# A mixing layer computed with seven block products per output pair instead of eight, its weight parts prepared one stage earlier

## The chip, the cores and the metric

The kernel runs on one core of one Trainium2 chip. The core has TensorE (PE: matrix products into PSUM), VectorE (DVE), ScalarE (ACT), GpSimd (POOL) and SyncE (SP, which here only issues DMAs). The metric is the device time of one execution in microseconds. The kernel before takes 1331.76 us, the median of three runs (1331.52 to 1332.87).

## The reference

One decoder layer over 1024 tokens of width 1024, in float32:

```python
xn = rmsnorm(x, norm_mix_w)
proj = xn @ w_in                       # q, k, v of both attentions, two gates
y_da = diff_attention(...)             # (1024, 512)
y_sw = sliding_window_attention(...)   # (1024, 512)
merged = sigmoid(g_da) * (y_da @ w_br_da) + sigmoid(g_sw) * (y_sw @ w_br_sw)
x = x + merged @ w_mix_out             # the mixing layer: 1024 x 1024 x 1024
xn = rmsnorm(x, norm_ffn_w)
x = x + conv_ffn(xn, w_up, conv_w, conv_b, w_down)   # width 2816
return rmsnorm(x, norm_final_w)
```

The change touches the mixing layer, `merged @ w_mix_out`, the merge just before it and the first step of the up projection just after it.

## The kernel before, in words

Everything is kept transposed: a tile has 128 channels on the partitions and up to 1024 tokens along the free dimension, so the width of 1024 makes eight tiles. TensorE works on float32r operands. To keep float32 accuracy each factor is split into a high part (a cast on ACT, float32 to float32r) and a low part (a subtraction on DVE, value minus high part), and each product of two blocks costs three matmuls: high x high, high x low, low x high.

Large products are mostly computed with a seven-product scheme (Strassen-Winograd form): both factors are cut into 2 x 2 blocks, sums and differences of blocks are formed, seven block products are computed instead of eight, and the results are recombined. The input projection, the up projection (`hidden`) and the down projection (`down`) do this. In the down projection the sums of weight blocks are formed by DMA: a tile `S` is loaded on SP's queue, negated on ACT (L108) where needed, and further quarters are added to it by an accumulating DMA on POOL's queue (L91). The mixing layer before the change uses plain products.

**The merge** (`rest`, from L781). Eight input tiles `y` from the two attentions are split. Then, for each output tile m = 0..7 (loop at L802): the branch weights of tile m are taken from a queue of prepared weights (`next_w`, which keeps two sets: cast L156 on ACT, subtraction L158 on DVE); two gate tiles `gr` are loaded from DRAM (four buffers), multiplied by the norm factor on POOL (L808), put through the sigmoid on ACT (L815); TensorE computes both branches, 48 matmuls, into a two-bank tile `sc` and two one-bank tiles `g`; DVE multiplies them into the gates (L819, L824); POOL adds the two (L825; DVE for the last tile); ACT and DVE split the sum into `mh` and `ml` (L828, L829).

**The mixing layer** (`mix`, L842). For each of eight output tiles: the residual tile `x` is loaded, the split weights are taken from the queue, 48 matmuls go to `sc` (L177 to L179, `mm3`), DVE adds the residual (L867), the sum is stored for later use (`x2d`), ACT scales it by the next norm's weight (L870) and squares it (L879), POOL adds the squares up (L880). After every second tile, `operands` (L886) forms the block operands of the up projection from the pair of tiles k and k+4.

**The first step of the up projection** (`hidden`, L922). For j = 0 five of the seven products run over the first three k, then the last operands T4 and T2 are split, then the five products get their fourth k, with column sums of the squares behind them, and the remaining two products follow.

The order of the work on each engine is made by the framework's scheduler from the program order, priorities (`high_priority`) and the dependencies; each engine then runs its own list strictly in order, and so does each DMA queue. A tile pool with `bufs=n` lets n tiles of one tag live at the same time.

## Time and profile before

The profile is of one execution that took 1330.42 us, with a span of 1328.4 us from its first to its last instruction.

| | us | share of the span |
|---|---|---|
| one profiled execution | 1330.42 | |
| its span | 1328.4 | |
| TensorE busy | 1315.8 | 99% |
| VectorE busy | 1049.4 | 79% |
| ScalarE busy | 614.7 | 46% |
| GpSimd busy | 478.0 | 36% |
| the merge, 500 to 588 us: TensorE / VectorE / ScalarE / GpSimd busy | 88.0 / 47.2 / 33.4 / 57.2 | |
| the mixing layer, 588 to 675 us: the same | 87.0 / 52.1 / 34.0 / 24.3 | |

A row of the groups by line reads: line of the kernel, engine, operation, output <- inputs, shape, number of instructions | busy us in total, mean ns of one | idle us of the engine just before them, and what ended most of it. A row of the timeline reads: start in us, length in us, engine, line, operation, count, and in brackets the idle time before it and what ended it. A row of the chain reads: start, length, engine and line of the piece of work on the path that ended last. The rows of windows give for each stretch its length, then for PE, PEld, DVE, ACT and POOL the busy us with the number of instructions, then the granted clock, the mean busy share of the 16 DMA engines and GB/s. Matmuls are pipelined, so the length of one row is longer than the distance to the next.

### The profile page before, as it was taken

To read this page: it belongs to the slowest core of one execution; us is meant where nothing else is said; L and a number is where in the kernel's file an instruction comes from. 1 tells how busy PE (TensorE), PEld (TensorE's weight loads), DVE (VectorE), ACT (ScalarE), POOL (GpSimd) and SP (SyncE) were. 2 spreads that over 40 slices of the span, in tenths; PEclk is the share of its full clock that TensorE was granted. 3 is DMA by queue.
4 is the path that set the end of the run, shared out by engine and by line. 5 is a ranking of instruction groups with operands and counts; after the bars stand their busy time and mean duration, and the time that the engine had idled before them with its cause. 6 is when DMAs were issued, how large, how long until landed. Compare 5 with 4: busy or idle time off the path is not lost.

```text
span 1328.4 us, 17040 instructions
## 1 busy us (share of the span) xinstructions
PE 1315.8 (99%) x6264; PEld 1097.6 (83%) x6264; DVE 1049.4 (79%) x1431; ACT 614.7 (46%) x946; POOL 478.0 (36%) x364
## 2 busy tenths in 40 slices
PE   9999999999999999999999999999999999999997
PEld 7888888888888878888888888888888888888886
DVE  8846775289888976455669999999999997886654
ACT  9432232276667774333444443343434344345643
POOL 0446652001101015751435666665566631101111
PEclk9999999999999999999999999999999999999999
DMA  7334333966554236334422222122222228867532
GB/s 260 126 144 157 145 148 122 269 179 190 143 133 142 82 126 225 120 118 151 143 95 95 80 79 93 66 95 80 82 77 86 81 75 333 266 158 143 111 98 108
DMA packets 63234, 180.25 MB, mean 136 GB/s; under 512 B 6960, under 2 KB 16816, under 8 KB 63152
## 3 DMA queue, kind: packets, MB, share of 16 engines
q1 hardware_dynamic: 49120, 153.48, 35.1%
q0 software_dynamic: 2304, 8.39, 3.7%
q10 hardware_dynamic: 11728, 17.31, 3.6%
q8 instruction: 49, 0.80, 0.3%
q14 instruction: 33, 0.27, 0.1%
HBM read 130.39 MB, written 48.76 MB: 135 GB/s over the span
## 4 chain that ended last, share of the span: by engine, by line
PE 97%; ACT 1%; DVE 1%; DMA 0%; issue 0%; SPq 0%; POOLq 0%; POOL 0%; ACTq 0%
PE t L919 45%; PE y L1169 7%; PE d L1169 5%; PE g L177 4%; PE g L178 4%; PE g L179 4%; PE sc L177 3%; PE sc L179 3%; PE sc L178 3%; PE sc L651 3%; PE y L1120 2%; PE d L1120 2%; PE t L667 1%; PE t L770 1%; PE sc L739 1%; PE t L679 1%
## 5 line engine op out<-in xcount | busy, mean ns | idle before, releaser
L1063 POOL TENSOR_TENSOR us<-us,rstd 128x1024 f32<-128x1024 f32 x42 | 92.2, 2214 | 82.5 <-DVE us L484 47.6
L1072 ACT ACTIVATE c<-us,vecs 128x1024 f32<-128x1024 f32 x44 | 54.8, 1248 | 127.1 <-POOL us L1063 121.5
L137 DVE TENSOR_TENSOR sl<-sf,sh 128x1024 fp32r<-128x1024 f32 x62 | 89.3, 1441 | 12.8 <-ACT sh L135 12.8
L158 DVE TENSOR_TENSOR wl<-raw,wh 128x1024 fp32r<-128x1024 f32 (+1 forms) x49 | 68.0, 1389 | 35.5 <-ACT wh L156 25.9
L135 ACT CAST sh<-sf 128x1024 fp32r<-128x1024 f32 x62 | 64.6, 1044 | 62.1 <-PE t L919 44.0
L156 ACT CAST wh<-raw 128x1024 fp32r<-128x1024 f32 (+1 forms) x49 | 49.6, 1014 | 91.2 <-PE sc L178 33.4
L121 POOL TENSOR_TENSOR sf<-rv 128x512 f32<-128x512 f32 x30 | 50.4, 1679 | 99.5 <-DVE sl L137 59.0
L1169 PE MATMUL y<-h,wh 128*128 128x512 f32 (+1 forms) x288 | 80.8, 366 | 0.0
L1075 DVE SCALAR_TENSOR_TENSOR c<-us,vecs,c 128x1024 f32<-128x1024 f32 x44 | 78.5, 1817 | 0.0
L1074 DVE SCALAR_TENSOR_TENSOR c<-us,vecs,c 128x1024 f32<-128x1024 f32 x44 | 69.3, 1606 | 5.6 <-ACT c L1072 5.5
L123 POOL TENSOR_TENSOR sf<-raw,rv 128x512 f32<-128x512 f32 x30 | 56.7, 1890 | 46.6 <-DVE sl L137 46.6
L177 PE MATMUL g<-xh,wh 128*128 128x512 f32 x176 | 71.0, 404 | 1.5 <-ACT g L580 1.5
L178 PE MATMUL g<-xl,wh 128*128 128x512 f32 x176 | 70.3, 400 | 0.0
L179 PE MATMUL g<-xh,wl 128*128 128x512 f32 x176 | 70.2, 399 | 0.0
L1055 ACT ACTIVATE c<-c 128x1024 f32<-128x1024 f32 x22 | 23.4, 1063 | 83.4 <-DVE c L1075 83.4
L655 DVE CUSTOM_DVE_ANT_0 L<-sc,bias 128x128 f32<-128x128 f32 (+7 forms) x64 | 47.7, 752 | 17.0 <-PE sc L651 13.7
L634 POOL MEMSET aT<- 128x128 f32 x32 | 6.1, 204 | 151.8 <-PE t L680 98.0
L137 DVE TENSOR_TENSOR wl<-raw,wh 128x1024 fp32r<-128x1024 f32 (+1 forms) x32 | 59.7, 1864 | 0.1
L1169 PE MATMUL d<-h,wh 128*128 128x512 f32 x192 | 59.4, 390 | 0.0
L1169 PEld LDWEIGHTS y<-h,wh 128*128 128x128 f32 x288 | 52.1, 189 | 8.7
L122 POOL TENSOR_TENSOR sf<-sf,raw 128x512 f32<-128x512 f32 x31 | 58.2, 1878 | 2.2
L656 ACT ACTIVATE L<-L,sm 128x128 f32<-128x128 f32 (+7 forms) x64 | 49.6, 778 | 20.0 <-DVE sm L655 17.3
(411 smaller groups left out, 4255.4 us busy)
## 6 DMA issues: line engine op xcount, KB each, us to landing
u<-qd SPq DMA_DIRECT2D x72, 256.0 KB, 6.4
raw<-in_w_up SPq DMA_DIRECT2D x23, 512.0 KB, 3.5
raw<-in_w_in SPq DMA_DIRECT2D x22, 512.0 KB, 3.7
hd<-c SPq DMA_DIRECT2D x22, 512.0 KB, 2.6
rv<-in_w_up SPq DMA_DIRECT2D x21, 512.0 KB, 3.6
gr<-gd SPq DMA_DIRECT2D x16, 512.0 KB, 3.4
S<-in_w_down POOLq DMA_DIRECT2D x16, 512.0 KB, 6.7
qd<-us SPq DMA_DIRECT2D x15, 512.0 KB, 2.6
```

Of the source, the lines that this page charges most:

```text
L122: tt(sa[:, 1], sa[:, 0], g[:, 0], ALU.subtract)
L135: cast = nc.scalar.copy(hi, src)
L137: low = nc.vector.tensor_tensor(lo, src, hi.bitcast(F32), ALU.subtract)
L158: self.lo = (eng or nc.vector).tensor_tensor(wl, raw, wh.bitcast(F32), ALU.subtract)
L177: nc.tensor.matmul(ps, wh[:, kc + o, :], ah, start=first and n == 0, stop=False)
L178: nc.tensor.matmul(ps, wh[:, kc + o, :], al, start=False, stop=False)
L179: nc.tensor.matmul(ps, wl[:, kc + o, :], ah, start=False, stop=last and n == len(kcs) - 1)
L919: nc.tensor.matmul(ps, (ah, ah, al)[p][:, k, :], (bh, bl, bh)[p], start=first and n == p == 0, stop=last and p == 2 and n == len(ks) - 1, ...
L1063: i = (nc.vector if m % NF == 0 else nc.gpsimd).tensor_tensor(us[:, 2:], us[:, 2:], self.rstd, ALU.mult)
L1074: nc.vector.scalar_tensor_tensor(c, us[:, 1:T + 1], cw[1], c, ALU.mult, ALU.add)
L1075: nc.vector.scalar_tensor_tensor(c, us[:, 0:T], cw[0], c, ALU.mult, ALU.add)
L1169: nc.tensor.matmul(ps, v[:, k, :], x, start=start and k == i == 0, stop=k == 7 and i == 2, skip_group_check=True)
```

## The change

The mixing layer now uses the seven-product scheme too. `w_mix` is cut into quarters; the weight operands of the seven products (in the order P1, P2, P5, P6, P3, P7, P4) are made during the merge, two "parts" after each of the merge's tiles 0 to 6. A part covers two of the four output pairs: 128 x 1024 values. Parts of P1, P2 and P4 are plain quarters, loaded from DRAM (`raw_part`). Parts of P5, P6, P3 and P7 come from two running tiles (`es`) that are loaded, accumulated by DMA on POOL's queue, and negated on ACT between products; for P3 they are loaded afresh. Each part is split (cast on ACT, subtraction on DVE) and both halves are stored to a DRAM buffer `pd` on SP's queue at the start of the next tile. `fetch_part` reads them back before their product: two parts at the end of the merge, one more among the residual loads, then one each two products of a stage ahead.

The merge's sum goes, unsplit, to tiles `mr`; for m < 4 its left half is split at once as P1's operand; for m >= 4 a difference of halves is formed. `mix` runs the seven products as stages over four output pairs, 12 matmuls for each, into eight PSUM banks (tags `d` and `y`) that are kept across stages. The residual tiles are all loaded at its start. `prep` forms the operands of the coming stage, `evict` adds a finished bank to the residual, and `ready` forms and splits the up projection's operands as tiles become complete. In `hidden`, j = 0 now computes four products whole (P1, P5, P3, P7), then the column sums, then P6, P2 and P4.

```diff
-        self.mix_order = [m for k in range(4) for m in (k, k + 4)]
-        src += [(self.w_mix[m], KC) for m in self.mix_order]
...
+                for mp_ in range(2):
+                    self.raw_part(mp_, False, False)
                 for m in range(KC):
+                    while self.parted:
+                        self.parted.pop(0)()
                     w = self.next_w()
...
+                    x = self.mr[m]
+                    (nc.vector if m == KC - 1 else nc.gpsimd).tensor_tensor(x, gs[0], gs[1], ALU.add)
+                    if m < 4:
+                        o = self.tl(op0, [P, 2, H2], "o0", F32R)
+                        self.B["P1", m] = self.split(o[:, 0], o[:, 1], x[:, :H2])
+                    else:
+                        x = self.mr[m - 4]
+                        nc.vector.tensor_tensor(x[:, :H2], x[:, H2:], x[:, :H2], ALU.subtract)
+                    for u in (2 * m, 2 * m + 1):
+                        if u < 14:
+                            self.part(u)
+                    if m in (0, 5):
+                        for mp in range(2):
+                            self.raw_part(mp, True, m > 0)
+                    if m == KC - 1:
+                        self.mw = {}
+                        for u in range(2):
+                            self.fetch_part(u)
...
+    def part(self, u):
+        nc, name, mp = self.nc, MIXING[u // 2], u % 2
+        flat = lambda t: t.rearrange("p (m k) c -> p m (k c)", m=2)
+        add = lambda s, *q: nc.gpsimd.dma_start(flat(s), self.mixing(mp, *q), accum_op=ALU.add)
+        if name in ("P1", "P2", "P4"):
+            s = self.raws.pop(0)
+        else:
+            s = self.S[mp]
+        hi, lo = (self.tl(self.ep, [P, KC, P], t, F32R) for t in ("eh", "el"))
+        self.split(hi, lo, s)
+        if name == "P1":
+            t = self.tl(self.ep, [P, KC, P], "es")
+            self.S.append(t)
+            nc.sync.dma_start(flat(t), self.mixing(mp, False, True))
+            add(t, True, True)
+        elif name in ("P5", "P6", "P3"):
+            if name == "P3":
+                nc.sync.dma_start(flat(s), self.mixing(mp, False, True))
+            def turn():
+                if name != "P6":
+                    nc.scalar.mul(s, s, -1.0)
+                add(s, name == "P6", False)
+            self.parted.append(turn)
+        for i, t in enumerate((hi, lo)):
+            self.parted.append(lambda i=i, t=t: nc.sync.dma_start(self.pd[u, i], t.bitcast(F32).rearrange("p k c -> p (k c)")))
...
+            plan = {"P1": (1, True, 0, 0, False), "P2": (0, True, 0, 0, True), "P5": (0, True, 4, 1, False), "P6": (1, False, 0, 1, False),
+                    "P3": (0, False, 0, 1, True), "P7": (1, False, 4, 1, True), "P4": (1, False, 4, 0, True)}
...
+            for i, name in enumerate(MIXING):
+                which, start, o, hf, done = plan[name]
+                for m in range(4):
+                    if m % 2 == 0:
+                        u = 2 * i + m // 2
+                        wh, wl = self.mw.pop(u)
+                        if 2 < u + 2 < 14:
+                            self.fetch_part(u + 2)
...
+                    for k in range(4):
+                        h, l = B[name, k]
+                        for p, (v, x) in enumerate(((wh, h), (wh, l), (wl, h))):
+                            nc.tensor.matmul(ps, v[:, m % 2 * 4 + k, :], x, start=start and k == p == 0, stop=k == 3 and p == 2, skip_group_check=True)
...
+                    if name == "P4" and m:
+                        for n in ("B22", "T3", "T2"):
+                            ready(n, m - 1)
+                    for f in owed:
+                        f()
...
-                    for name, a, b in prods[:5]:
+                    for n in (0, 2, 4, 3):
+                        name, a, b = prods[n]
                         ps[name] = self.tl(psF, [P, H2], "t")
-                        self.product(ps[name], w[a], b, range(3), last=False)
+                        self.product(ps[name], w[a], b)
```

More of the change, by code (lines that the diff above doesn't have):

```diff
@@ L837, in split, with fetch_part @@
+    def fetch_part(self, u):
+        tags = ("raw", "raw") if u in (0, 3, 6, 9) else ("wh", "wl")
+        r = []
+        for i, tag in enumerate(tags):
+            t = self.tl(self.wp, [P, KC, P], tag, F32R, **({"bufs": RAW} if tag == "raw" else {}))
+            self.nc.sync.dma_start(t.bitcast(F32).rearrange("p k c -> p (k c)"), self.pd[u, i])
+            r.append(t)
+        self.mw[u] = r
     def split(self, hi, lo, src, eng=None):
@@ L947, in hidden @@
                     ssq = self.tl(psF, [P, H2], "t")
[L948 to L953 removed]
+                    self.col_sums(ssq, [self.rstd], NB, 0)
+                    with tc.high_priority(400):
+                        rs = self.rstd_cols(ssq, 8, D)
                 if j == NF - 1:
@@ L961, in hidden @@
                         lo = self.lo
[L962 removed]
+                for name, a, b in (prods[i] for i in ((0, 1, 2, 5, 3, 6, 4) if j == NF - 1 else (0, 1, 2, 5, 3, 4, 6) if j else (5, 1, 6))):
                     if name not in ps:
```

174 lines of the change are left out of this document (105 added, 69 removed).

## The prediction

> **What bounds the kernel now.** I read the page first, then the chain that ended last, then the stages by window, then the lines inside two stages, then the DMAs.
>
> ```profile
> span 1328.4 us, 17040 instructions
> PE 1315.8 (99%) x6264; PEld 1097.6 (83%) x6264; DVE 1049.4 (79%) x1431; ACT 614.7 (46%) x946; POOL 478.0 (36%) x364
> q0 software_dynamic: 2304, 8.39, 3.7%
> PE 97%; ACT 1%; DVE 1%; DMA 0%; issue 0%; SPq 0%; POOLq 0%; POOL 0%; ACTq 0%
> ```
>
> ```profile
> 674.93 13.61 PE t L919 x60
> 688.54 1.68 PE t L185 x16
> 1162.60 21.76 PE y L1169 x96
> ```
>
> ```profile
> 500.00:588.00 88.00, 88.00 (x390) 72.88 (x389) 47.23 (x39) 33.36 (x33) 57.24 (x21) 1.00 0.43 161
> 588.00:675.00 87.00, 87.00 (x386) 72.04 (x385) 52.14 (x48) 33.99 (x44) 24.27 (x17) 1.00 0.42 137
> ```
>
> ```profile
> 500.00:512.00 12.00, 12.00 (x54) 9.95 (x53) 9.58 (x8) 7.01 (x8) 6.64 (x2) 1.00 0.94 365
> ```
>
> TensorE carries 97% of the chain. One 512-column matmul costs 21.76/96 = 0.2267 us. The merge (500 to 588) and the mixing layer (588 to 675) have no TensorE idle time at all, so the change can win only by removing matmuls, and loses whatever waits it puts into these two stages. The columns of the window rows are PE, PEld, DVE, ACT, POOL, clock, DMA share, GB/s: the spare room is on DVE (41 us), POOL (31 us) and the DMA engines, except in the merge's first 12 us, where DMA is at 0.94.
>
> How close the merge is to its limits shows in its lines and its order in time:
>
> ```profile
> L808 POOL TENSOR_TENSOR gr<-gr,rstd 128x1024 f32<-128x1024 f32 x14 | 35.5, 2537 | 37.7 <-DMA gr<-gd 37.5
> L825 POOL TENSOR_TENSOR gr<-gr,gr 128x1024 f32<-128x1024 f32 x7 | 22.6, 3235 | 1.0 <-ACT wh L156 1.0
> L158 DVE TENSOR_TENSOR wl<-raw,wh 128x1024 fp32r<-128x1024 f32 x8 | 19.0, 2380 | 15.0 <-ACT wh L156 15.0
> L815 ACT ACTIVATE gr<-gr 128x1024 f32<-128x1024 f32 x15 | 15.9, 1061 | 36.3 <-POOL gr L808 36.3
> L824 DVE TENSOR_TENSOR gr<-gr,g 128x512 f32<-128x512 f32 x14 | 9.2, 683 | 5.6 <-PE g L179 5.6
> L156 ACT CAST wh<-raw 128x1024 fp32r<-128x1024 f32 x8 | 8.3, 1040 | 2.7 <-PE g L178 2.7
> ```
>
> ```profile
> L158 DVE TENSOR_TENSOR wl<-raw,wh 128x1024 fp32r<-128x1024 f32 x7 | 8.5, 1219 | 0.0
> L839 DVE TENSOR_TENSOR B_0l<-xw,B_0h 128x512 fp32r<-128x512 f32 x3 | 2.0, 684 | 1.5 <-ACT B_0h L838 1.5
> L838 ACT CAST B_0h<-xw 128x512 fp32r<-128x512 f32 x3 | 1.7, 607 | 0.0
> ```
>
> ```profile
> 500.69 0.39 PE L177 MATMUL sc<-yh,wh 128*128 128x512 f32 x1
> ```
>
> ```profile
> 556.49 2.40 POOL L808 TENSOR_TENSOR gr<-gr,rstd 128x1024 f32<-128x1024 f32 x1 [3.48 <-DMA gr<-gd]
> 561.93 3.37 POOL L825 TENSOR_TENSOR gr<-gr,gr 128x1024 f32<-128x1024 f32 x1
> 568.68 2.40 POOL L808 TENSOR_TENSOR gr<-gr,rstd 128x1024 f32<-128x1024 f32 x1 [3.38 <-DMA gr<-gd]
> ```
>
> ```profile
> 523.51 2.27 DVE L158 TENSOR_TENSOR wl<-raw,wh 128x1024 fp32r<-128x1024 f32 x1 [0.17 <-ACT wh L156]
> 573.15 1.58 DVE L158 TENSOR_TENSOR wl<-raw,wh 128x1024 fp32r<-128x1024 f32 x1 [3.18 <-ACT wh L156]
> ```
>
> TensorE needs 48 x 0.2267 = 10.88 us per tile m, from 500.69. POOL's round is already 568.68 - 556.49 = 12.2 us. The weights for m=3 are split by 525.8 and needed at 533.3 (7.5 us of slack); those for m=7 by 574.7, needed at 576.8 (2.1 us). The merge lives on a shrinking lead. Any round above 12.2 us becomes TensorE idle time before the end.
>
> **The change, part by part.** *Removed.* Eight tiles of 8 x 2 x 3 matmuls are 384; seven products of 4 x 4 x 3 are 336. 48 x 0.2267 = -10.9 us, all on the path. This is the whole gain.
>
> *Added to the merge.* Fourteen weight parts, two per tile: on ACT 14 full casts (1.04) and 4 sign changes, on DVE 14 full subtractions (1.22), on POOL 8 accumulating DMAs; in exchange the full split of the merged tile becomes a half split and a half difference (0.68 each). The split sizes are cheap. Their places in the queues are not. In the changed program's instruction order DVE has, per tile: the three gate products, low of part one, half split, half difference, low of part two, and only then the low half of the weights for tile m+2. ACT has the sign changes and both casts ahead of the next weights' cast. POOL no longer runs its two gate products one tile ahead of the sum: they stand behind the accumulating DMAs, which wait for ACT's sign change or DVE's subtraction. On SP the gate loads stand behind the four stores of the preceding parts, so behind DVE.
>
> Prices for the accumulating chain come from the down projection, which does the same:
>
> ```profile
> L91 POOL DMA_DIRECT2D S<-in_w_down x16: 856/866/1105, 1153.8 to 1247.5; - x16
> DMA to landing us min/median/max: 5.4/6.7/11.6
> ```
>
> ```profile
> L106 SPq DMA_DIRECT2D S<-in_w_down x4: 328/330/333, 1224.6 to 1240.9; - x4
> DMA to landing us min/median/max: 3.4/4.6/5.1
> ```
>
> Now tile by tile. Weights for m=3: 525.8 today, plus four subtractions (4 x 1.22), four half operations (4 x 0.68) and one wait for POOL's sum (2.4) is 535.8; the third matmul needs them at 533.8. Late by 2.0.
>
> Weights for m=4, one round later, from DVE's last part to the next: sign change 1.06 (taken as a sigmoid), issue 0.87, two gate products 4.8, sigmoid 1.06, two products 1.36, sum 3.37, half cast 0.61, part's cast 1.04, weights' cast 1.04, subtraction 1.22: 16.4, less the 3.3 us by which the previous weights stood behind the part (sign change, cast, subtraction): 13.1. Excess over 10.9: 2.2. With the sum at its undisturbed 2.4 the excess is 1.2.
>
> Weights for m=5: the same without the sign change, and with only 1.22 to take off: 14.2, excess 3.3 (2.3 with the short sum).
>
> Weights for m=6: part P3 overwrites its tile by a fresh load, negates it, adds to it, and P7's cast waits for all that, ahead of the weights' cast: 4.6 + 1.06 + 0.87 + 6.7 + 1.04 + 1.04 + 1.22 - 1.22 = 15.3. With the shortest landings 12.8, with the longest 20.7. The merge will have more traffic than the down projection, and the second accumulate stands behind POOL's sum, so I take 17.8: excess 6.9.
>
> After that (P7 to P4) the parts come from plain loads and the lead returns. Lag of the merge: 2.0 + 2.2 + 3.3 + 6.9 = 14.4 us. Ends: 0 (short sums and landings, 5.4 of excess, eaten by the 7.5 us of slack) and 2.0 + 2.2 + 3.3 + 9.8 = 17.3 with the longest landings, or the DMA bound below, 23.
>
> *Mixing layer.* TensorE needs 336 x 0.2267 = 76.2 us. DVE there: 28 evictions, 24 operand lows, 8 differences, 36 half steps for the next layer at 0.68, and the first pair's 4.3 (3 x 1.22 + 0.68): about 70 us against 52 now. It fits, but in the last stage each product brings four steps and an eviction, 3.4 us beside TensorE's 2.7, so DVE arrives late. Part fetches run 5.4 or 10.9 us ahead against a landing of 4.6: 1 us for these (0 to 3).
>
> The eight residual loads move to the stage's start, 8 x 1.35 = 10.8 us of DMA (price below), behind the first parts in SP's queue; the first is used one product later, and P1 as a whole (10.9) hides them. If a backlog of the merge stands ahead, they come out of the same 0 to 3.
>
> ```profile
> 674.97 1.22 DVE L867 TENSOR_TENSOR x<-x,sc 128x1024 f32<-128x1024 f32 x1 [4.21 <-PE sc L179]
> 688.87 1.22 DVE L839 TENSOR_TENSOR T_3l<-xw,T_3h 128x1024 fp32r<-128x1024 f32 x1
> ```
>
> *Handover.* After the last matmul DVE has an eviction and four steps (3.4) before the low half of S1/S2 (1.2): ready at 4.8, while TensorE asks at 3.6 (P1 and four more). Stall 1.2 at least, up to 6 if DVE comes in late by the 2 to 4 us of the stage before and POOL's sums delay it. The tail on DVE, 674.97 to 690.1 today, is 15.1 us; five products with their column sums (13.61 + 1.68) just covered it, four leave 12.6. I take 3.5.
>
> Sum: -10.9 + 14.4 + 1.0 + 3.5 = **+8.0 us**. The profiled execution took 1330.42 us (its span and 2.0 around it), 1.3 below the median of the runs, 1331.76. So 1338.4 on the profile's scale, 1339.8 on the median's: **1340**.
>
> **Rivals.** *All of it hides (faster).* If landings stay at 3.4 and 5.4 us and the early slack holds, the merge keeps pace and only part of the handover is paid: 1331.8 - 10.9 + 1.2 = 1322. For it: the 41 us of free DVE, 0.43 DMA share. Against: the order of the queues. It decides at a mean round of 12.2 us. 15%.
>
> *The DMA engines become the bound.* The stage's transfers now:
>
> ```profile
> gr<-gd SPq DMA_DIRECT2D x12, 512.0 KB, 3.3
> raw<-in_w_br SPq DMA_DIRECT2D x4, 512.0 KB, 4.2
> raw<-in_w_mix SPq DMA_DIRECT2D x4, 512.0 KB, 4.1
> x<-in_xT SPq DMA_DIRECT2D x2, 512.0 KB, 9.1
> ```
>
> In 500 to 512 us they moved 365 GB/s at 0.94, so 512 KB cost 0.524/0.388 = 1.35 us of all engines; an accumulate costs 0.037 x 1328.4/16 = 3.07 us (16 transfers make the 8.39 MB). The merge uses 0.43 x 88 = 37.8 us now; it gains 28 stores, 10 reads and 4 fetches, and loses 6 loads (the last two rows): 36 x 1.35 = 48.6, and 8 x 3.07 = 24.6. Together 111 us for an 88 us stage: lag 23, or about 12 if the last stores spill past it. With 23: 1331.8 - 10.9 + 23 + 4.5 = 1348. 28%. [...]
>
> *DVE and POOL exclude each other, and nothing else binds.* The same subtraction takes 2380 ns beside POOL in the merge and 1219 in the mixing layer. Serialised, a round has POOL 7.2 and DVE 3 x 1.22 + 2 x 0.68 = 5.0: 12.2 us, 1.3 over TensorE, for seven rounds 9, less 2 of slack: 1331.8 - 10.9 + 7 + 3.5 = 1331. 12%. [...]
>
> **How the numbers follow.** My forecast 40%, DMA bound 28%, exclusion alone 12%, hidden 15%, and 5% for a late fetch inside the mixing layer on top (up to 1360). Range 1325 to 1357: it leaves out half of the hidden case and a few per cent above. What a measurement here can tell from no change is about 0.2%, 2.7 us. Faster 0.19 (hidden and a third of exclusion), same 0.07, slower 0.74.
>
> **What would show it.** Right: TensorE idle time in the merge released by DVE or ACT weights' lines, the largest at m=6; its last matmul about 14 us later than 587.7; the stage after it 76 us plus little; a stall near the second product of the next layer. DMA bound: share of 0.9 through the merge and gate loads landing at 6 us or more instead of 3.3. Wrong: no idle time before m=6, or P3's chain shorter than 11 us.

## The result and the profile after

The changed kernel takes 1391.82 us, median of 4 runs (1389.86 to 1393.65); the kernel before, run beside it, 1331.64 us. The ratio is 1.0452, 95% interval 1.0430 to 1.0474: 60 us slower, where 1340 us (1325 to 1357) had been predicted. The profiled execution took 1393.65 us.

The page of the changed kernel, the rows that answer those shown of before:

```profile
span 1391.8 us, 17229 instructions
...
PE 1326.7 (95%) x6216; PEld 1099.8 (79%) x6216; DVE 1086.4 (78%) x1497; ACT 639.8 (46%) x989; POOL 486.9 (35%) x372
...
q0 software_dynamic: 4480, 12.58, 5.1%
...
PE 82%; DVE 6%; issue 5%; POOL 3%; DMA 2%; ACT 2%; SPq 0%; POOLq 0%; ACTq 0%; DVEq 0%
```

TensorE runs 48 matmuls fewer (10.9 us at 0.2267) and yet is busy 10.9 us longer, so the remaining ones took 21.8 us more; its idle time went from 12.6 to 65.1 us. -10.9 + 21.8 + 52.5 = +63.4, the difference of the spans. "issue" has 5% of the chain, 0% before.

The stages by window, changed kernel: merge, mixing layer, 47 us of handover to the up projection, the rest. Columns as in the prediction (length; PE, PEld, DVE, ACT, POOL busy; clock, DMA share, GB/s):

```profile
500.80:637.00 136.20, 100.33 (x386) 78.69 (x385) 69.19 (x57) 45.27 (x48) 64.85 (x29) 0.85 0.86 284
637.00:717.00 80.00, 78.19 (x337) 63.88 (x335) 61.63 (x82) 36.33 (x63) 23.89 (x15) 0.98 0.71 255
717.00:764.00 47.00, 32.36 (x122) 25.04 (x122) 34.18 (x40) 20.83 (x30) 20.54 (x17) 0.82 0.25 84
764.00:1391.80 627.80, 619.65 (x2800) 515.32 (x2798) 541.35 (x545) 267.79 (x319) 255.58 (x181) 0.99 0.37 115
```

The kernel before, from the end of its mixing layer:

```profile
674.80:701.80 27.00, 27.00 (x132) 22.72 (x131) 20.90 (x21) 14.49 (x18) 12.06 (x11) 1.00 0.23 83
701.80:1328.40 626.60, 618.54 (x2791) 513.36 (x2789) 549.37 (x552) 263.77 (x321) 262.61 (x185) 1.00 0.38 116
```

The merge takes 136.2 us instead of 87.2 (+49), the mixing layer 80.0 instead of 86.9 (-7), and from there to the end it is 674.8 instead of 653.6 (+21). So there are two losses, in the merge and in the handover.

TensorE in the merge, in order of time; the bracket is the idle time ahead of the matmul and its releaser:

```profile
532.40 0.80 PE L178 MATMUL g<-yh,wh 128*128 128x512 f32 x1 [4.21 <-DVE gr L831]
...
558.52 0.80 PE L178 MATMUL g<-yh,wh 128*128 128x512 f32 x1 [10.89 <-DVE gr L831]
559.11 0.63 PE L179 MATMUL g<-yl,wh 128*128 128x512 f32 x1
559.54 0.63 PE L180 MATMUL g<-yh,wl 128*128 128x512 f32 x1
...
576.35 0.80 PE L178 MATMUL g<-yh,wh 128*128 128x512 f32 x1 [4.20 <-DVE gr L831]
...
588.29 0.50 PE L180 MATMUL sc<-yh,wl 128*128 128x512 f32 x1 [3.03 <-DVE wl L159]
...
589.19 0.63 PE L180 MATMUL sc<-yh,wl 128*128 128x512 f32 x1
...
611.55 0.79 PE L178 MATMUL sc<-yh,wh 128*128 128x512 f32 x1 [10.94 <-ACT wh L157]
```

The first three of these stalls, in the third to fifth tile, are not for weights: TensorE waits for the PSUM bank that VectorE's gate product (line 831) has to empty. After the long stalls the matmuls follow each other by 0.43 us (559.11 to 559.54) instead of 0.2267; the granted clock is 0.50 there (558.5 to 561.2 us) and 1.00 again from 562 to 571. Behind 4.20 us of idle time a matmul takes 0.80 us, behind 3.03 us 0.50. But the fourth matmul behind those 3.03 us is slow too (0.63 at 589.19, with the clock at 0.50 from 589.2 to 592), so the length of one gap does not settle it here.

What the gate product waits for is on POOL: in the fourth tile VectorE waits 13.19 us for ScalarE's sigmoid, and that 13.36 us for POOL's product. POOL in the same stage; L868 is the accumulating DMA, L815 the product of gate and reciprocal root:

```profile
538.37 1.21 POOL L868 DMA_DIRECT2D es<-in_w_mix  x1 [2.92 <-ACT es L886]
550.76 1.22 POOL L868 DMA_DIRECT2D es<-in_w_mix  x1 [11.18 <-issue]
551.52 5.13 POOL L815 TENSOR_TENSOR gr<-gr,rstd 128x1024 f32<-128x1024 f32 x2
...
587.87 1.21 POOL L868 DMA_DIRECT2D es<-in_w_mix  x1 [2.45 <-ACT es L886]
...
599.20 1.22 POOL L868 DMA_DIRECT2D es<-in_w_mix  x1 [6.17 <-issue]
```

The second accumulating DMA of a pair stands for up to 11.18 us although nothing in the profile releases it ("issue"), and the gate products for the next tile stand behind it. That is a wait that the prediction did not have. The group of the eight accumulates, issue in ns and landing in us:

```profile
L868 POOL DMA_DIRECT2D es<-in_w_mix x8: 1194/1218/1388, 511.2 to 599.2; - x8
...
DMA to landing us min/median/max: 5.8/9.9/12.1
```

The handover, TensorE:

```profile
720.46 0.50 PE L1044 MATMUL t<-o,wl 128*128 128x512 f32 x1 [2.22 <-DVE wl L138]
...
730.24 1.22 PE L1044 MATMUL t<-o,sh 128*128 128x512 f32 x2 [7.21 <-ACT sh L136]
...
753.15 0.96 PE L1044 MATMUL t<-o,wh 128*128 128x512 f32 x3 [1.86 <-ACT wh L136]
...
756.97 0.80 PE L1044 MATMUL t<-o,wl 128*128 128x512 f32 x1 [2.86 <-DVE wl L138]
```

### The profile page after: what moved, and what is told of

Read it like the earlier page. It is cut to its first block, busy times and chain, and to the rows that moved or that the text cites. A ratio compares the mean times of both kernels' runs of the same rounds, so it can differ in the third digit from the quotient of the medians.

```text
span 1391.8 us, 17229 instructions
## 1 busy us (share of the span) xinstructions
PE 1326.7 (95%) x6216; PEld 1099.8 (79%) x6216; DVE 1086.4 (78%) x1497; ACT 639.8 (46%) x989; POOL 486.9 (35%) x372
## 4 chain that ended last, share of the span: by engine, by line
PE 82%; DVE 6%; issue 5%; POOL 3%; DMA 2%; ACT 2%; SPq 0%; POOLq 0%; ACTq 0%; DVEq 0%
PE t L1044 41%; PE y L1292 6%; PE d L1292 5%; PE g L178 3%; PE g L179 3%; PE g L180 3%; PE sc L651 3%; PE d L1243 2%; PE y L1243 2%; DVE o L905 1%; PE t L667 1%; POOL gr L815 1%; PE t L770 1%; PE d L1006 1%; POOL mr L833 1%
## 5 line engine op out<-in xcount | busy, mean ns | idle before, releaser
L1044 PE MATMUL t<-o,sh 128*128 128x512 f32 x528 | 164.7, 394 | 7.2 <-ACT sh L136 7.2
L1044 PEld LDWEIGHTS t<-o,sh 128*128 128x128 f32 x528 | 100.1, 190 | 28.8 <-ACT sh L136 8.1
L136 ACT CAST sh<-sf 128x1024 fp32r<-128x1024 f32 x62 | 65.1, 1051 | 91.8 <-PE t L1044 71.1
L1044 PE MATMUL t<-o,sl 128*128 128x512 f32 x264 | 103.3, 392 | 0.0
L1044 PE MATMUL t<-o,wh 128*128 128x512 f32 x352 | 101.0, 396 | 2.3 <-ACT wh L136 2.3
L1044 PEld LDWEIGHTS t<-o,wh 128*128 128x128 f32 x352 | 67.2, 191 | 17.2 <-ACT wh L136 3.2
L159 DVE TENSOR_TENSOR wl<-raw,wh 128x1024 fp32r<-128x1024 f32 (+1 forms) x41 | 53.2, 1300 | 25.8 <-ACT wh L157 16.1
L157 ACT CAST wh<-raw 128x1024 fp32r<-128x1024 f32 (+1 forms) x41 | 41.2, 1007 | 64.2 <-PE y L1243 15.2
L1044 PE MATMUL t<-o,wl 128*128 128x512 f32 x176 | 60.2, 397 | 5.1 <-DVE wl L138 5.1
L138 DVE TENSOR_TENSOR wl<-raw,wh 128x1024 fp32r<-128x1024 f32 (+1 forms) x32 | 59.7, 1866 | 0.5
```

The source lines that it names most:

```text
L136: cast = nc.scalar.copy(hi, src)
L138: low = nc.vector.tensor_tensor(lo, src, hi.bitcast(F32), ALU.subtract)
L1044: nc.tensor.matmul(ps, (ah, ah, al)[p][:, k, :], (bh, bl, bh)[p], start=first and n == p == 0, stop=last and p == 2 and n == len(ks) - 1, ...
```

## The experiments

The theories: 1, the second accumulate waits on POOL for room that `dynamic_dma_scratch_size` (1024 here) sets and that the rows of the first one fill (the theory calls it room for descriptors; the trace shows the wait, not what fills); 2, the DMA engines are full; 3, the chain of reload, sign change, accumulate and cast ahead of part P7; 4, the clock that falls after idle time; 5, the handover's own order and memory. All runs in one table (us; merge, mixing layer and the rest from the profiled execution, by windows cut as above; "head" is the time ahead of the merge, 501 to 503 where it isn't given):

| kernel | time | ratio to before | merge | mixing | rest |
|---|---|---|---|---|---|
| before | 1331.64 | 1 | 87.2 | 86.9 | 653.6 |
| changed | 1391.82 | 1.0452 | 136.2 | 80.0 | 674.8 |
| rows4k | 1377.60 | 1.0349 [1.0334, 1.0365] | 121.6 | 80.2 | 674.4 |
| ring2k (head 507.8) | 1394.20 | 1.0478 [1.0461, 1.0496] | 122.3 | 77.5 | 683.7 |
| pads (head 507.0) | 1410.46 | 1.0594 [1.0576, 1.0612] | 136.1 | 78.8 | 684.3 |
| nostore | 1382.81 | 1.0387 [1.0372, 1.0403] | 128.1 | 76.8 | 674.0 |
| rows_nostore | 1362.93 | 1.0236 [1.0219, 1.0253] | 111.0 | 76.3 | 672.6 |
| rows_noacc | 1365.74 | 1.0257 [1.0242, 1.0273] | 112.6 | 76.3 | 674.3 |
| fill | 1397.93 | 1.0504 [1.0488, 1.0520] | 145.0 | 76.3 | 673.9 |
| onepart | 1340.49 | 1.0068 [1.0053, 1.0083] | 87.0 | 77.9 | 672.6 |
| sqfree | 1392.90 | 1.0464 [1.0448, 1.0480] | 136.2 | 80.1 | 675.3 |
| p2first | 1372.34 | 1.0308 [1.0293, 1.0324] | 121.2 | 78.6 | 668.8 |
| hand | 1372.05 | 1.0298 [1.0282, 1.0313] | 120.7 | 78.7 | 668.2 |
| hand2 | 1367.38 | 1.0271 [1.0256, 1.0286] | 121.7 | 78.7 | 663.9 |
| one_hand2 | 1331.94 | 1.0006 [0.9997, 1.0016] | 87.1 | 78.3 | 663.9 |
| best | 1356.65 | 1.0180 [1.0165, 1.0195] | 108.1 | 82.3 | 660.1 |
| best2 | 1356.29 | 1.0188 [1.0171, 1.0205] | 108.6 | 83.5 | 660.6 |

Five of these runs multiply by wrong weights in the mixing layer: nostore and rows_nostore leave out most of the bytes of 24 stores, rows_noacc leaves out the accumulates, onepart and one_hand2 leave out twelve of the fourteen parts. They measure time alone.

In the edited kernels line numbers move by a few: L867 or L868 is the accumulating DMA in all of them.

**The wait on POOL: rows4k, ring2k, pads.** First, half as many rows for the same bytes:

```diff
     def mixing(self, mp, right, below):
-        m = 2 * mp + 4 * below
-        return self.w_mix[m:m + 2, :, 4 * right:4 * right + 4, :].rearrange("m p k c -> p m (k c)")
+        return self.w_mix[int(below), mp, int(right)]
...
-        "w_mix": _chunks(a(w_mix_out)[0]),
+        "w_mix": np.ascontiguousarray(_chunks(a(w_mix_out)[0]).reshape(2, 2, 2, P, 2, 4, P).transpose(0, 1, 4, 3, 2, 5, 6)).reshape(2, 2, 2, P, 2, 4 * P),
```

> Only the layout of the mixing weights in DRAM differs: each quarter that the parts read is contiguous, so a partition's share is one row of 4 KB instead of two of 2 KB. Bytes, instructions and their order are those of the changed kernel (1391.8 us). Theory 1 (the second accumulating DMA of each pair waits on POOL for room among the descriptors of the first; POOL's gate products stand behind it): half as many rows fit, POOL's waits of 5 to 11 us ahead of the second accumulate go, and with them TensorE's stalls of 4.2, 10.9 and 4.2 us in front of the gated products (line 178, released by DVE's gate product); 19 us of idle time and some 8 of slow clock behind it: about 1365. Theory 2 (the 16 DMA engines are full): the bytes are the same, so 1387 to 1392. Theory 3 (the reload, sign change and accumulate ahead of part P7): its stall of 10.9 us at the seventh tile stays under both.

POOL's accumulates in this run, and its merge:

```profile
538.85 0.88 POOL L867 DMA_DIRECT2D es<-in_w_mix  x1 [2.85 <-ACT es L885]
540.69 0.88 POOL L867 DMA_DIRECT2D es<-in_w_mix  x1 [0.96 <-ACT es L885]
```

```profile
501.90:623.50 121.60, 97.32 (x385) 77.02 (x384) 72.86 (x57) 45.80 (x48) 65.11 (x29) 0.89 0.90 311
```

The second accumulate goes out 1.84 us after the first (12.4 us before), the stalls of 10.89 and 4.20 us in front of line 178 are gone, and the merge is 14.6 us shorter. Theory 1's direction holds; its size (27 us) does not, since other stalls took part of the room: 3.5 and 4.9 us for the fourth tile's weights, 4.7 for the sixth's, 4.0 and 2.4 for the seventh's. And of the 4.21 us in front of the third tile's gated products 2.80 stayed: there POOL's product waited 9.02 us for the gate load (at 527.84), not for room. The same test by the setting, with the rows as they were:

```diff
-LPAD, RPAD = 480, 480
+LPAD, RPAD = 16, 16
...
-    nc = _bacc.Bacc("TRN2", target_bir_lowering=False, num_devices=1, dynamic_dma_scratch_size=1024)
+    nc = _bacc.Bacc("TRN2", target_bir_lowering=False, num_devices=1, dynamic_dma_scratch_size=2048)
```

> The changed kernel with twice the room for POOL's descriptors (2048 instead of 1024 bytes a partition; two unused pads are cut from 480 to 16 bytes for it). The transfers themselves are untouched. Theory 1 (room for descriptors): the second accumulates issue without a wait, as in the run with 4 KB rows, about 1365. Theory 2 (DMA engines full): 1387 to 1392. If 4 KB rows help and this does not, the gain was the transfers' shape and not the room.

The total did not move, but the merge did: by 13.9 us, with the transfers in their old shape.

```profile
545.33 1.20 POOL L868 DMA_DIRECT2D es<-in_w_mix  x1 [2.86 <-ACT es L886]
547.16 1.22 POOL L868 DMA_DIRECT2D es<-in_w_mix  x1 [0.63 <-ACT es L886]
```

```profile
507.80:630.10 122.30, 97.66 (x386) 77.63 (x385) 74.26 (x57) 45.81 (x48) 66.12 (x29) 0.87 0.95 316
```

The gain was given back ahead of the merge (+7) and behind the handover (+9). The control has the first line of the diff alone:

> Control for the run with more room for descriptors (1394.2 us: its merge was 14 us shorter than the changed kernel's, but the stages before it took 7 us more and those behind the handover 9 us more). Here only the two unused pads are cut from 480 to 16 bytes, the room stays at 1024. If the shifted addresses made the other stages slower: 1391.8 + 16 = 1405 to 1409, with the merge at 136. If the larger room itself did it: 1390 to 1393.

It took 1410.46 us, with the merge at its 136:

```profile
507.00:643.10 136.10, 100.74 (x385) 79.06 (x384) 69.59 (x57) 45.26 (x48) 64.90 (x29) 0.85 0.86 282
```

So the loss outside the merge belongs to the pads (with the same setting and the same work, pads cut by 464 bytes cost 18.6 us; why was not tried), and the setting alone is worth 16.3 us, 13.8 of it in the merge. The wait went twice: with half the rows for the same bytes (from 12.39 us between the two accumulates to 1.84; q0 moved 1152 packets instead of 2176 from 500 to 640 us) and with the setting doubled (1.83, with the 2176 packets as they were). Both agree with theory 1, though no trace shows the room itself; what it is worth is 14 to 16 us, not 27.

**The DMA engines: nostore, rows_nostore, rows_noacc.** 24 stores cut to an eighth:

```diff
-            self.parted.append(lambda i=i, t=t: nc.sync.dma_start(self.pd[u, i], t.bitcast(F32).rearrange("p k c -> p (k c)")))
+            self.parted.append(lambda i=i, t=t: nc.sync.dma_start(*((self.pd[u, i], t.bitcast(F32).rearrange("p k c -> p (k c)")) if u < 2 else (self.pd[u, i, :, :P], t[:, 0].bitcast(F32)))))
...
-            self.nc.sync.dma_start(t.bitcast(F32).rearrange("p k c -> p (k c)"), self.pd[u, i])
+            self.nc.sync.dma_start(t.bitcast(F32).rearrange("p k c -> p (k c)"), self.pd[u % 2, i])
```

> 24 of the 28 stores of the weights' parts are cut to an eighth (the first 128 columns of each partition's row), and all parts are fetched back from those of the first pair, so the mixing layer multiplies by wrong weights; every instruction and every fetch stays. By 1.35 us for 512 KB that takes 24 x 7/8 x 1.35 = 28 us of the 16 DMA engines' time out of the merge. Theory 2 (DMA engines full): the merge's 135 us fall by 20 to 28, total 1364 to 1372. Theory 1 (room for descriptors on POOL): the second accumulates still wait, only for a faster first one: 0 to 8 us, total 1384 to 1392.

The same on top of the 4 KB rows:

> The run with 4 KB rows (1377.6 us; its merge 121.6 us with the DMA engines at 0.90) and also 24 of the 28 stores of parts cut to an eighth, so the mixing layer multiplies by wrong weights; instructions and fetches stay. Beside the short run of stores alone (1382.8) it tells whether, once POOL no longer waits for descriptors, the DMA engines bind. Theory 2 (they do): 28 us less of DMA time shorten the merge by 15 to 25 us, total 1353 to 1363. Theory 3 (the chain of reload, sign change, accumulate, cast and split binds): the stalls stay where they are, 1372 to 1377.

And the 4 KB rows without the accumulates (`add = lambda s, *q: None`):

> The run with 4 KB rows (1377.6 us) without POOL's eight accumulating DMAs: the running sums are not formed, parts P5, P6, P3 and P7 are split from what the plain loads and sign changes leave, so the output is wrong. It takes away 8 x 3.07 = 24.6 us of DMA time and eight landings of 6 to 12 us in front of casts. Theory 2 (DMA engines): like the run with the stores cut, 15 to 22 us faster, 1355 to 1362. Theory 3 (latency of the chain): at least the 6.4 us of stall at the seventh tile and 4.7 at the fifth go, and the clock behind them, more than the cut stores bring: 1355 to 1365, while the cut stores bring under 5.

Their merges, in this order:

```profile
503.00:631.10 128.10, 100.73 (x386) 80.59 (x385) 77.00 (x56) 46.60 (x50) 64.99 (x29) 0.87 0.77 231
```

```profile
500.90:611.90 111.00, 95.23 (x386) 76.87 (x385) 73.65 (x55) 46.62 (x49) 64.88 (x29) 0.92 0.85 264
```

```profile
502.10:614.70 112.60, 95.18 (x385) 75.66 (x384) 73.73 (x58) 47.17 (x51) 58.40 (x21) 0.92 0.84 313
```

While POOL still waits (up to 10.05 us ahead of an accumulate in nostore), the cut stores shorten the merge by 8 us (nostore, at 1382.81 us, is just under theory 1's 1384 to 1392 and far from theory 2's 1364 to 1372). Without that wait they shorten it by 10.6, and 3.9 more come in the mixing layer, which then has no stall (76.3 us, against 336 x 0.2267 = 76.2). Taking away the accumulates instead gives about the same (9.0 and 3.9). The cuts of 28 and 24.6 us are worked out; share times length in the windows gives a merge in which the DMA engines are busy for 94 and 95 us instead of 109, so 15 us less in both. The two cut about the same amount and different work on POOL, ACT and the chain of P7; theory 2 asked for just that. But about two thirds of the 15 us come back, and rows_noacc missed theory 2's range by 4 us. Theory 3, that the chain of P7 binds, does not hold in this form: with the stores cut and the chain left as it was, the stalls of 4.0 and 2.4 us for the seventh tile's weights are gone. With the stores cut TensorE still idles 15.8 us of the merge, all of it ahead of gated products. That past the DMA engines the order of the work on each engine is the next limit is the reading of these stalls; it was not tried.

**The clock: fill.** Needless matmuls into the idle time:

```diff
+                    self.fill({6: 44}.get(m, 0), parts)
                     ps = self.tl(self.psS, [P, T], "sc")
                     self.mm3_both(ps, w, yact[0], range(4))
                     nc.vector.tensor_tensor(gs[0], gs[0], ps, ALU.mult)
+                    self.fill({2: 16, 3: 44, 4: 16}.get(m, 0), parts)
                     for hf in range(2):
...
+    def fill(self, n, parts):
+        if n:
+            ps = self.tl(self.psT, [P, H2], "t")
+            for i in range(n):
+                self.nc.tensor.matmul(ps, parts[i % 8][0][:, :P], parts[i % 8][0][:, :H2], start=i == 0, stop=i == n - 1)
```

> The changed kernel with 120 needless matmuls (into a spare PSUM bank, of operands long there) put where TensorE stands idle in the merge: 16 ahead of the gated products of the third and fifth tile, 44 ahead of those of the fourth, 44 ahead of the seventh tile. At 0.2267 us they are 27 us of work in 30 us of idle time. Theory 4 (the granted clock falls because TensorE stood idle, and real matmuls pay for it afterwards): the clock of the merge rises from 0.85 to over 0.95, the 382 matmuls there take about 88 us instead of 99, and the kernel is 5 to 12 us faster, about 1383, although it does more work. If the clock has another reason (load, the DMA traffic): no gain, 1391 to 1397.

```profile
500.80:645.80 145.00, 121.41 (x505) 97.14 (x505) 66.16 (x58) 47.33 (x51) 63.44 (x29) 0.93 0.85 280
```

```profile
583.30 0.79 PE L178 MATMUL g<-yh,wh 128*128 128x512 f32 x1 [7.44 <-DVE gr L833]
...
606.82 0.79 PE L178 MATMUL g<-yh,wh 128*128 128x512 f32 x1 [9.70 <-DVE gr L833]
```

The clock half of theory 4 holds here: with TensorE's idle time in the merge down from 35.9 to 23.6 us the granted clock went from 0.85 to 0.93, and 121.41 - 120 x 0.2267 = 94.2 us are left for the real matmuls, 6.1 less. The time half stays open. The merge is 8.8 us longer, and the stalls moved to the fifth and sixth tile; but the needless matmuls were not all in idle time. Ahead of the seventh tile its weights were ready (the low half at 611.8) before the 44 needless matmuls began, and its own matmuls waited for these until 624.06:

```profile
610.46 1.37 DVE L159 TENSOR_TENSOR wl<-raw,wh 128x1024 fp32r<-128x1024 f32 x1 [3.09 <-ACT wh L157]
```

```profile
614.08 10.13 PE L861 MATMUL t<-yh 128*128 128x512 f32 x44
```

That is about 10 us of the edit's own making, more than the loss. VectorE's order changed too: in the fifth tile two subtractions of parts (4.77 us) ran ahead of the gate product. What the trace does show is the fourth tile: the third tile's last gated matmul started at 538.04 instead of 540.23, 2.2 us earlier, and the gate product that the fourth tile waits for came only 0.3 us earlier (557.44 instead of 557.77). That stall does not wait for TensorE's speed. What the slow clock costs in the merge as a whole no run shows.

**The handover: onepart, sqfree, p2first, hand, hand2, one_hand2.** First the change without the merge's cost:

```diff
                     for u in (2 * m, 2 * m + 1):
-                        if u < 14:
+                        if u < 2:
                             self.part(u)
-                    if m in (0, 5):
-                        for mp in range(2):
-                            self.raw_part(mp, True, m > 0)
...
-            self.nc.sync.dma_start(t.bitcast(F32).rearrange("p k c -> p (k c)"), self.pd[u, i])
+            self.nc.sync.dma_start(t.bitcast(F32).rearrange("p k c -> p (k c)"), self.pd[u % 2, i])
```

> The changed kernel in which the merge makes only the first two of the fourteen parts (no accumulates, no reloads, none of the other casts, subtractions and stores); the mixing layer fetches those two again and again, so its output is wrong, but all its work and the handover stay. It takes the merge's cost out and shows the mixing layer and the handover alone. The merge is back at about 88 us and the mixing layer at 77. Theory 5 (the handover to the up projection costs about 21 us by its own order and memory): 1331.3 + 1 - 10 + 21 = 1343. If the handover only pays for the merge's backlog and for a clock lowered there: 3.5 us of it stay, 1322 to 1326.

```profile
500.60:587.60 87.00, 87.00 (x385) 72.06 (x384) 42.76 (x43) 29.68 (x32) 54.46 (x21) 1.00 0.63 236
587.60:665.50 77.90, 76.71 (x337) 62.80 (x336) 63.08 (x84) 36.82 (x63) 25.60 (x16) 1.00 0.65 226
```

The merge is the old one, the mixing layer saves 9.0 us, and the rest costs 672.6 - 653.6 = 19.0. Theory 5: the handover loses more by itself than the whole change can save. The first suspect was memory. In the changed kernel the cast that ends the stall of 7.21 us was released by POOL's addition to the sum of squares:

```profile
729.14 1.04 ACT L136 CAST sh<-sf 128x1024 fp32r<-128x1024 f32 x1 [1.63 <-POOL rstd L980]
```

```diff
-                    sq = self.tl(sqp, [P, H2], "sq")
+                    sq = self.tl(sqp, [P, H2], "sq") if preps else half(mr[4 + m % 4], hf)
```

> The changed kernel (1391.8 us) with the squares of the last three stages put into halves of merged tiles that nobody reads any more, instead of four buffers of their own. In the memory map the first buffer of the up projection's sums (the one that the cast of line 136 fills) lies on top of two of those four buffers, so that cast had to wait for POOL's last addition to the sum of squares. Theory 5a (this overlap makes the handover's stall of 7.2 us): the two casts go some 10 us earlier, the stall falls to at most 3, 1384 to 1388. Theory 5b (VectorE, busy without a gap from 700 to 738 us, is the bound and the casts only happen to end last): another VectorE line takes the stall over, 1390 to 1392.

The stall of 7.21 us became 0.53, and the kernel is not faster. TensorE and POOL there:

```profile
741.74 0.59 PE L186 MATMUL t<-ones,rstd 128*128 128x1 f32 x2 [6.46 <-POOL rstd L980]
```

```profile
731.94 9.74 POOL L980 TENSOR_TENSOR rstd<-rstd,mr 128x512 f32<-128x512 f32 x1 [4.96 <-ACT mr L979]
```

The last addition took 9.74 us, while VectorE ran subtractions without a gap, and the column sums waited 6.46 us for it. The last of VectorE's row is this one; the addition ended at 741.68, 1.1 us behind it:

```profile
739.35 1.21 DVE L905 TENSOR_TENSOR T_2l<-t,T_2h 128x1024 fp32r<-128x1024 f32 x1
```

So the overlap in memory was real, and removing it uncovered the next wait. Then the second pair, on the 4 KB rows:

```diff
-... else (5, 1, 6))):
+... else (1, 5, 6))):
```

> The run with 4 KB rows (1377.6 us), and behind the column sums of the first pair the product P2 (A12) comes ahead of P6 instead of behind it. The second pair's cast needs the buffer that A11 and A12 share, and in the changed kernel that is held until P2 is through, at the end of the pair. Theory 5c (the two stalls of 1.85 and 2.85 us at the second pair come from that buffer): they go, 1371 to 1374. If POOL's late sums (they start behind the column sums) are what the second pair waits for: 1376 to 1378.

```profile
735.83 0.73 PE L1043 MATMUL t<-o,wh 128*128 128x512 f32 x2 [0.90 <-ACT wh L136]
...
738.28 0.50 PE L1043 MATMUL t<-o,wl 128*128 128x512 f32 x1 [1.72 <-DVE wl L138]
```

5.3 us, as theory 5c had it; 1.85 and 2.85 us of stall became 0.90 and 1.72, so they shrank but did not go. With the two other changes beside it (the squares as in sqfree, and the last addition on VectorE):

```diff
-                    nc.gpsimd.tensor_tensor(half(acc, hf), half(acc, hf), sq, ALU.add)
+                    (nc.vector if (m, hf) == (KC - 1, 0) else nc.gpsimd).tensor_tensor(half(acc, hf), half(acc, hf), sq, ALU.add)
```

> The run with 4 KB rows (1377.6 us) with three changes in the handover: the squares in dead halves of merged tiles (so the sums' buffer lies under nothing that POOL still reads), the last addition to the sum of squares on VectorE instead of POOL (it took 9.74 us on POOL in the run with the squares moved, beside an unbroken row of VectorE instructions, against 1.3 us alone), and P2 ahead of P6. Theory 5 (these three places make the handover's stalls of 6.0, 1.9 and 2.9 us): 10 to 14 us with the clock behind them, 1364 to 1368. If VectorE's work itself (busy without a gap from 700 to 738 us) is the bound: at most 5 us, 1372 to 1377.

0.3 us beyond p2first, within the spread: the 10 to 14 us of theory 5 did not come, and the time is where the rival (VectorE's work, 1372 to 1377) had it. The stall moved once more:

```profile
734.04 1.08 PE L1043 MATMUL t<-o,wh 128*128 128x512 f32 x2 [4.07 <-ACT wh L136]
```

```profile
726.49 0.10 POOL L1184 MEMSET us<- 128x2 f32 x1 [15.38 <-DVE T_3l L904]
726.59 1.67 POOL L195 TENSOR_TENSOR rs<-ms,mhalf 128x8 f32<-128x8 f32 x1
```

The clearing of two columns of the result tile waits 15.4 us for VectorE; the reciprocal root stands behind it on POOL, and the second pair's sums are held until that is issued. Both are taken away:

```diff
-                    with nullcontext() if j else tc.issue_after(self.pow.ins):
+                    with nullcontext():
...
-        nc.gpsimd.memset(us[:, 0:2], 0.0)
+        (nc.gpsimd if m % NF else nc.vector).memset(us[:, 0:2], 0.0)
```

> The run with the three changes in the handover (1372.05 us, with stalls of 1.4, 2.3, 4.1 and 1.8 us left) and two more: the second pair's sums on POOL are no longer held back until the reciprocal root behind the column sums is issued, and the clearing of two columns of each first half's result tile is on VectorE instead of POOL (there it stood ahead of that reciprocal root and waited 15.4 us for VectorE). Theory 5d (the second pair is late because its sums wait in POOL's order behind the column sums): the stalls of 4.1 and 1.8 us go, 1364 to 1367. If the casts wait for buffers or VectorE instead: 1370 to 1373.

4.7 us for the two together, nearly what theory 5d had (1364 to 1367); they were not tried apart. And without the merge's cost:

> The run with only two of the fourteen parts made (1340.5 us: merge as before, mixing layer 78 us, handover and rest 19 us more than before; its output is wrong in the same way), with the five changes in the handover. It asks whether the mixing layer's saving of 9 to 11 us would reach the end if the parts cost nothing. Theory 5 (order and memory of the handover, which these changes mend in part): 10 to 15 us less, 1326 to 1331, at or below the kernel before. If VectorE's work in the last mixing stage is the bound: 1334 to 1340.

Handover of hand2, then the last stretch of both:

```profile
701.30:748.30 47.00, 40.21 (x172) 31.85 (x173) 46.61 (x54) 27.96 (x39) 24.28 (x13) 0.93 0.24 79
748.30:1365.20 616.90, 609.05 (x2750) 506.46 (x2748) 534.70 (x539) 259.63 (x312) 254.75 (x179) 0.99 0.39 116
```

```profile
713.30:1330.20 616.90, 609.08 (x2750) 506.49 (x2748) 534.57 (x539) 259.49 (x312) 254.30 (x179) 0.99 0.39 116
```

Handover and rest take 663.9 us with the merge's load and without it, so the merge's backlog is no part of them. Of the 21 us (20.8 with 4 KB rows), 5.6 were P2's place, 4.3 POOL's order and 0.6 the rest of hand; 10.3 stay, in a stretch where VectorE is busy 46.6 of 47 us. That VectorE's work is what binds there is the reading of hand2's first row; it was not tried by taking work off it. With 1331.94 us, just above what theory 5 had, the change, freed of twelve of its fourteen parts, only draws level with the kernel before.

**The fastest: best, best2.** P2 and P4 need no sums, so they can be split where they are used, on top of hand (best) and hand2 (best2):

```diff
+LATE = (2, 3, 12, 13)
...
-                        if u < 14:
+                        if u not in LATE and u < 14:
                             self.part(u)
-                    if m in (0, 5):
-                        for mp in range(2):
-                            self.raw_part(mp, True, m > 0)
...
         r = []
+        if u in LATE:
+            s = self.tl(self.wp, [P, KC, P], "raw", bufs=RAW)
+            self.nc.sync.dma_start(s.rearrange("p (m k) c -> p m (k c)", m=2), self.mixing(u % 2, True, u > 3))
+            self.mw[u] = self.split(*(self.tl(self.wp, [P, KC, P], tag, F32R, **({"bufs": RAW} if tag == "raw" else {})) for tag in tags), s)
+            return
```

> The handover's three changes and 4 KB rows, and the four parts of P2 and P4, which are plain quarters of the weights, are no longer made in the merge: they are loaded in the mixing layer and split there, as the kernel before did with all its mixing weights. That takes 8 stores and 4 loads (16 us of DMA time) and 4 casts and subtractions out of the merge and 4 transfers out of the mixing layer, and adds 4.9 us of VectorE and 4.2 us of ScalarE there. Theory 2 (DMA engines bind the merge once POOL's wait is gone): the merge falls from 121.6 to about 107, the total to 1348 to 1354; still slower than before, since the ten remaining parts and eight accumulates are 95 us of DMA in 87. If VectorE in the mixing layer overflows: stalls there, 1355 to 1365.

> The fastest run that computes the reference (1356.65 us: 4 KB rows, P2 and P4 split in the mixing layer, three changes in the handover) with the two further changes. Its second pair still had stalls of 1.1 and 0.8 us and its handover and rest took 6.7 us more than before: 1353 to 1356 by theory 5d; no gain if something else is late there.

```profile
500.90:609.00 108.10, 91.87 (x385) 73.69 (x384) 63.41 (x52) 42.20 (x44) 62.53 (x29) 0.94 0.89 299
```

The merge fell from 120.7 to 108.1 us, as the DMA time promised (107); the mixing layer took 3.6 us of that back in stalls for the late splits. best2 is no faster than best (1356.29 against 1356.65): its rest is 660.6 against 660.1, so the POOL order of theory 5d no longer binds there. No version beats the kernel before.

## Why the prediction was wrong, point by point

*The gain.* Right: where the mixing layer has no stall it takes 76.3 us, 336 x 0.2267.

Of the 55 us between the forecast and the measured difference of the spans (+8.0, +63.4), 34.6 lie in the merge, 3.0 in the mixing layer and 17.7 behind it.

*The merge, +14.4; measured +49.* The step that failed is the price of the accumulating chain, taken from the down projection, "which does the same". It does not do the same: there a partition's share is one row of 4 KB, here two of 2 KB. The page shows it: queue q0 had 2304 packets for 16 transfers before, 144 each, and has 2176 more for the eight new ones, 272 each: 128 more, a second row for each partition; with 4 KB rows (rows4k) the eight took 1152, 144 each. The time of the DMA engines was priced rightly: q0 took 17.4% of the 140 us from 500 to 640, 24.4 us, against 24.6. The issue cost 1.2 us instead of 0.87, and the second of each pair waited up to 11.2 us more; with it waited POOL's gate products, which the prediction had put behind the accumulates but at their own duration. That is about 14 us (14.6 in rows4k, 13.8 between pads and ring2k). The lags ahead of the seventh tile were foreseen as 2.0, 2.2 and 3.3 us for weights; they came as 4.2, 10.9 and 4.2 us for the gate product, and 3.0 for weights. The landing was taken at 6.7 us; its median in the merge was 9.9.

The second failure is that DMA traffic and queue order were held for rivals. They add up: the merge's DMA time, 111 us by the rival's sum, was 0.90 x 121.6 = 109 us once POOL no longer waited, and in the changed kernel the gate loads landed after 7.7 us at the median, over the 6 us that the prediction had named as this rival's sign. Of the 34.4 us of lag that are left then, 10.6 come back with the cut stores; the other 23.8 are, in that run, 15.8 us of stalls on the gate path and 8 us by which the matmuls took more than 0.2267 us each, at a granted clock of 0.92 in the merge.

The chain from P3 to P7 was right in place, not in size. Its excess of 6.9 us was 10.94: the second accumulate went out 11.3 us after the first (587.87, 599.20) and its part's cast, ahead of the weights' cast, came behind that:

```profile
609.50 1.05 ACT L904 CAST eh<-es 128x1024 fp32r<-128x1024 f32 x1 [9.50 <-DMA es<-in_w_mix]
```

*The mixing layer, +1.0.* Near: 80.0 - 76.2 = 3.8 us in the changed kernel, a stall of 1.8 us and 2.0 us of slower matmuls at a granted clock of 0.98; 1.7 in onepart.

*The handover, +3.5 (up to 6); measured +21, and 19 with the merge's load away.* This step alone decides the sign: onepart, with the merge's cost away, is still 0.7% slower than before. How 10.3 of the 21 us come about was not tried. The prediction counted VectorE's instructions between the last matmul and the low half of S1 and S2, at undisturbed durations. It did not ask which buffers the moved product P2 holds (5.3 us), nor what stands in POOL's order ahead of the second pair's sums (4.7 us), and it took VectorE's subtractions at 0.68 us where they took up to 1.78 beside POOL.

*The clock.* It was not priced. The mean granted clock was 0.975, against 0.998 before; TensorE's slow matmuls are 21.8 us of its busy time. How much of that is an extra cost, and not taken out of the next stall, stays open: the run with filled gaps paid for its own needless matmuls.

*The rivals.* The DMA engines were one of the limits, and in the kernel as changed not the first one. "All of it hides" and "exclusion alone" are out. That VectorE's and POOL's times add up, as the second of these has it for a whole round, the traces show in single pairs only: in the kernel before, POOL's product ran from 559.56 to 561.97 us, and VectorE's subtraction, begun at 560.96, took 2.09 us instead of 1.22. The range missed the time by 35 us because each loss was bounded as if the others left it alone.

## What to carry to other kernels

Before taking a price from another stage, compare the shape: rows per partition, transfers in flight and what stands behind them in the queue (here an accumulate took 1.2 us to issue instead of 0.87 and landed after 9.9 us instead of 6.7). Where two DMAs go out one behind the other on an engine that also computes, price a wait between them as well (here up to 11.18 us on POOL), and count whose work stands behind it. Where a stage was without idle time, ask of every moved product which buffers it now holds longer (P2: 5.3 us here), and look for the wait that a removed one uncovers (in sqfree 7.21 us became 0.53, and 6.46 us came up behind it).

## What the hardware showed that was not expected

- Two accumulating DMAs of two 2 KB rows a partition went out 12.4 us apart with `dynamic_dma_scratch_size` at 1024; with 4 KB rows they were 1.84 us apart, with 2048 for the setting 1.83. The larger setting cost nothing by itself: pads and ring2k agree within 1.3 us in every other stage.
- One addition of 512 columns took 9.74 us on POOL beside an unbroken row of VectorE subtractions; of the seven ahead of it from 704 us on five took 1.30 to 1.59 and two 3.41 together. Eleven VectorE instructions started after the addition did, and it ended 1.1 us after the last of them. What held it up no run tried.
- Cutting two unused pads by 464 bytes each, which moves the buffers, cost 18.6 us (6 us ahead of the merge and 9.5 us behind the mixing layer in the profiled executions), with the same instructions. Its cause stays open.
